# Attention with query tiles in pairs and values 512 queries wide, its order written out from the last linear head to the MLP

## The chip, the cores and the metric

The kernel runs on one core of one Trainium2 chip. The metric is the device time of one execution in microseconds (us). Before the change it was 739.01 us, the median of 3 runs (738.43 to 739.06). The engines are named as in the profile: PE (TensorE, matmuls), PEld (its weight loads), DVE (VectorE), ACT (ScalarE), POOL (GpSimd) and SP (SyncE, which here only starts DMA transfers). The five engines run side by side, each works through its own queue in order, and they wait for each other through semaphores. SBUF is the working memory, PSUM the memory that PE writes its results to.

## What is computed

One transformer block on 512 tokens of width 1024: a projection, two mixers side by side (a gated linear attention of 4 heads, and a softmax attention of 8 heads with a low-rank query and key-value path), an output projection, an MLP with a squared ReLU of width 4096, and a last normalisation. Everything is float32. Cut to what matters here:

```python
def reference(x, ...):
    n = rmsnorm(x, g_mix)
    (gq, gk, gv, gr, z_gf, z_gb, cq, ckv, kr, z_ma, z_mb) = split(n @ w_in)
    y_gla = gla_branch(gq, gk, gv, gr, z_gf, z_gb, ...)      # 4 linear heads
    y_mla = mla_branch(cq, ckv, kr, positions, ...)          # 8 softmax heads
    merged = sigmoid(z_ma) * y_gla + sigmoid(z_mb) * y_mla
    h = x + merged @ w_out
    m = rmsnorm(h, g_mlp)
    h = h + square(relu(m @ w_ff1)) @ w_ff2
    return rmsnorm(h, g_final)

def attend(qblk):                    # per head: 96 wide queries and keys, 128 wide values
    s = einsum('bhqd,bhkd->bhqk', qblk, kt)
    p = softmax(s, axis=-1)
    return einsum('bhqk,bhkv->bhqv', p, vt)
```

## The kernel before

**Arithmetic.** A float32 matrix product is made from three matmuls (`mm3`, L87): each operand is split into a high part (a rounded copy, made by ACT) and a low part (the difference, made by DVE or POOL), and high x high, high x low and low x high are added in PSUM. `split` and `split_scaled` (L92 to L98) make the two parts. So most steps appear as: PE writes a bank, ACT copies the high part, DVE subtracts, PE uses both. The names of the tiles end in h and l for the parts.

**Stages.** The first projections and three linear heads fill the time to about 255 us. Then come the last linear head, the latent products of the softmax attention, the gates zb5 to zb7 and the first unit of weights (L1310 to L1346); the attention loop over 8 heads with 4 query tiles of 128 queries each (L1369 to L1453); the output projection, written as seven products of 2x2 blocks (`wo_product`, tiles wox, wow, woz, L1790 to L1858); the row normalisation and transposes (tiles ms, mb, mr, mh, ml) that lead to the MLP; and the MLP, in four quarters of a first (f) and a second (g) product, with a table of places (`PLACES`) for its steps. `last_rows` (L1745) ends the kernel.

**The attention loop.** In turn n it makes the scores of tile n (`att_scores`, L1095: 3 matmuls of 512 keys into tile s, DVE's maximum top, ACT's exponential e with its sum tot), normalises a pair of tiles (`att_normalise`, L1110: DVE's reciprocal of tot, then ACT scales the even tile and DVE the odd one), transposes tile n-3 (`att_flip`, L1116: four transposes into tile tp, then the split into pT, high by ACT and low by DVE) and, every second turn, multiplies with the values (`att_values`, L1127). A pT tile holds 256 queries, so each head has two halves, and each of their matmuls is 256 queries wide. `merge` (L1143) then adds the head to the linear branch: DVE makes tb, POOL the halves mx and my. `up_units` (L1023) is a generator that makes the queries q, keys kbuf and values v of two heads (a pair) in between; q is one tile with high and low part side by side, and `rotary_rows` (L1044) copies the rotated rows into it with SP's transfers. The streamed weights of the output projection (tiles bo10, bo11, bo20 and so on, 1024 columns each) and the first operands for it (ga, gh, gl) are split between the turns.

**PSUM.** There are eight banks in two groups of four, under the tags at and mm. Scores and transposes use the at banks; the values, the latent products and half of the output projection the mm banks.

**Order.** The program is traced first and a scheduler then sets the order on each engine. Edges that need no semaphore pin it: `in_program_order` (L110) keeps the traced order on the engines named, and `goes_behind` (L125) puts one group behind another. Before, DVE and ACT follow the traced order up to the last linear head, PE up to the gates; from there to the output projection the scheduler decides, with some dozen `goes_behind` edges; from L1790 on, PE, ACT and DVE follow the traced order, POOL does from the attention loop on, and SP from the first step of the MLP on. `last_rows` is pinned on all engines by itself.

**The tail.** `last_rows` takes the last product in parts, and per row tile i: `out_first` squares one half on ACT, `out_mean` scales that sum on POOL, `out_gained` multiplies the right half by the gains on POOL, `out_square` squares the left half on ACT, `out_rstd` adds on DVE and takes the power -1/2 on POOL, `out_left` makes the left half on DVE, `out_right` scales the right one on ACT, and `out_store` sends both.

## Time and profile before

| What | us |
|---|---|
| median of 3 runs | 739.01 |
| the profiled execution, its own time | 739.02 |
| its span, first to last instruction | 737.3 |
| PE busy | 726.9 |
| DVE busy | 625.0 |
| ACT busy | 494.2 |
| POOL busy | 220.7 |

The span leaves out what lies around the program, some 1.7 us. Busy times of PE hold the modelled ends of matmuls, which overlap: a matmul is listed with 0.28 to 0.48 us though the next one starts sooner. How long PE is really held by one is read from the distance between two starts. "L88 PE MATMUL av<-pT,v" is an instruction of line 88 that writes tile av and reads pT and v; numbers in tile names are left out where many are grouped. An arrow in brackets names what ended an engine's idle time. The granted clock of PE was 0.998 of the full one.

### The profile page before, as it was taken

Reading aid. Unit: us, or ns where it says so; the run is one execution under the profiler, and the core shown is the slowest. Engines: PE = TensorE matmul, PEld = TensorE weight load, DVE = VectorE, ACT = ScalarE, POOL = GpSimd, SP = SyncE. Lnnn points to the kernel's source line nnn. Section 1 sums busy time; section 2 is a strip of 40 time slices with the busy share of each in tenths; the row PEclk is TensorE's granted clock in tenths of the full one; section 3 lists DMA queues with packets and bytes.
Section 4 is the critical chain, followed back from the end, with each engine's and each line's share of the span. In section 5 each row is a group of like instructions: output and inputs, shape, how many; then the busy total and the mean of one; then the engine's idle time right before and its main releaser. Section 6 shows DMA issues by size and latency. Waiting matters only on the chain.

```text
span 737.3 us, 11473 instructions
## 1 busy us (share of the span) xinstructions
PE 726.9 (99%) x4226; PEld 643.1 (87%) x4226; DVE 625.0 (85%) x861; ACT 494.2 (67%) x809; POOL 220.7 (30%) x284
## 2 busy tenths in 40 slices
PE   9999999999999999999999999999999999999995
PEld 7888888888888888899888899889988998899984
DVE  7777787889988788798898889998699869987896
ACT  7557465595696675988856879545874477537764
POOL 0732020243743724126852511200211012101215
PEclk9999999999999999999999999999999999999999
DMA  9849682431222324557978899862987088815773
GB/s 309 277 100 215 215 188 90 79 64 31 58 58 58 51 72 89 127 111 214 291 145 233 133 267 185 184 204 63 250 181 192 20 240 175 196 57 146 170 114 114
DMA packets 80520, 109.95 MB, mean 149 GB/s; under 512 B 15920, under 2 KB 34352, under 8 KB 80464
## 3 DMA queue, kind: packets, MB, share of 16 engines
q1 hardware_dynamic: 63088, 75.64, 32.9%
q0 software_dynamic: 17088, 33.30, 27.1%
q8 instruction: 33, 0.54, 0.3%
q10 hardware_dynamic: 288, 0.28, 0.1%
q14 instruction: 23, 0.19, 0.1%
HBM read 104.22 MB, written 2.10 MB: 144 GB/s over the span
## 4 chain that ended last, share of the span: by engine, by line
PE 88%; DVE 5%; issue 2%; POOL 2%; ACT 1%; DMA 1%; POOLq 0%; DVEq 0%; ACTq 0%
PE first L326 3%; PE tp L1122 2%; PE zb L88 1%; PE zb L89 1%; PE zb L90 1%; PE f2x L90 1%; PE f3x L90 1%; PE f1x L90 1%; PE f3x L89 1%; PE f2x L89 1%; PE f1x L89 1%; PE f1x L88 1%; PE f3x L88 1%; PE f2x L88 1%; PE av L89 1%
## 5 line engine op out<-in xcount | busy, mean ns | idle before, releaser
L1626 POOL DMA_DIRECT2D w<-in_w_ff x40 | 48.3, 1240 | 254.9 <-DMA w<-in_w_ff 139.3
L1102 DVE TENSOR_REDUCE top<-s 128x1 f32<-128x512 f32 x32 | 21.6, 682 | 4.9 <-PE s L90 4.7
L1107 ACT ACTIVATE e<-s,top 128x512 f32<-128x512 f32 x32 | 21.9, 687 | 3.5 <-DVE top L1102 2.6
L94 DVE TENSOR_TENSOR pT<-tp,pT 128x512 fp32r<-128x512 f32 x32 | 21.8, 682 | 2.4 <-ACT pT L93 2.0
L93 ACT ACTIVATE pT<-tp 128x512 fp32r<-128x512 f32 x32 | 19.0, 595 | 3.2 <-PE tp L1122 3.2
L1122 PE MATMUL tp<-ident,e 128*128 128x128 f32 x128 | 19.4, 274 | 0.0
L88 PE MATMUL av<-pT,v 128*128 128x256 f32 x64 | 19.1, 299 | 0.0
L90 PE MATMUL av<-pT,v 128*128 128x256 f32 x64 | 18.2, 285 | 0.0
L89 PE MATMUL av<-pT,v 128*128 128x256 f32 x64 | 18.1, 284 | 0.0
L1122 PEld LDWEIGHTS tp<-ident,e 128*128 128x128 f32 x128 | 15.2, 140 | 3.1 <-ACT e L1113 0.7
L94 POOL TENSOR_TENSOR qF<-qk,qF 128x512 fp32r<-128x512 f32 x4 | 6.6, 1641 | 37.6 <-ACT qF L93 37.6
L667 POOL DMA_DIRECT2D gvw<-in_w_in x4 | 4.8, 1230 | 38.7 <-DVE gvw L672 34.0
L667 POOL DMA_DIRECT2D zaw<-in_w_in x4 | 4.9, 1228 | 32.7 <-DVE zaw L672 28.0
L1628 DVE TENSOR_TENSOR w<-w,w 128x1024 f32<-128x1024 f32 x12 | 14.4, 1220 | 0.1
L980 POOL DMA_DIRECT2D w<-in_w_out x10 | 12.2, 1400 | 6.5 <-DVE bo60l L94 5.3
L88 PE MATMUL s<-kbuf,q 96*128 96x512 f32 x32 | 14.1, 439 | 0.0
L1153 POOL TENSOR_TENSOR mx<-tb,yg 128x256 f32<-128x256 f32 x8 | 7.7, 964 | 19.8 <-DVE tb L1150 13.9
L577 ACT ACTIVATE bds<-bd 128x512 f32<-128x512 f32 x4 | 2.4, 597 | 15.8 <-PE bd L555 15.8
L89 PE MATMUL s<-kbuf,q 96*128 96x512 f32 x32 | 12.6, 395 | 0.0
L90 PE MATMUL s<-kbuf,q 96*128 96x512 f32 x32 | 12.6, 393 | 0.0
L1113 ACT ACTIVATE e<-e,tot 128x512 f32<-128x512 f32 x16 | 11.6, 726 | 1.3 <-DVE tot L1112 1.3
L89 PEld LDWEIGHTS av<-pT,v 128*128 128x128 f32 x64 | 12.2, 191 | 0.2
(2156 smaller groups left out, 3250.4 us busy)
## 6 DMA issues: line engine op xcount, KB each, us to landing
w<-in_w_ff SPq DMA_DIRECT2D x48, 512.0 KB, 5.6
w<-in_w_ff POOLq DMA_DIRECT2D x40, 512.0 KB, 6.2
w<-in_w_out POOLq DMA_DIRECT2D x10, 512.0 KB, 8.3
grw<-in_w_in SPq DMA_DIRECT2D x8, 512.0 KB, 8.6
zaw<-in_w_in SPq DMA_DIRECT2D x8, 512.0 KB, 7.4
gvw<-in_w_in SPq DMA_DIRECT2D x8, 512.0 KB, 4.7
w<-in_w_out SPq DMA_DIRECT2D x16, 256.0 KB, 5.6
w220f<-in_w_ff SPq DMA_DIRECT2D x8, 512.0 KB, 6.2
```

Source lines behind the costliest of these rows:

```text
L88: nc.tensor.matmul(acc, lh, rh, start=start, stop=False, skip_group_check=onto)
L89: nc.tensor.matmul(acc, lh, rl, start=False, stop=False, skip_group_check=onto)
L90: nc.tensor.matmul(acc, ll, rh, start=False, stop=stop, skip_group_check=onto)
L93: nc.scalar.activation(hi, src, AF.Copy)
L94: rest.tensor_tensor(lo, src, raw(hi), op=ALU.subtract)
L326: nc.tensor.matmul(f_accs[i], a[:, i * P : (i + 1) * P], b, start=k == 0 and x == 0, stop=k == KD - 1 and x == 2)
L980: nc.gpsimd.dma_start(d, rows.rearrange("(k t p) w -> p t k w", t=2, p=P)[:, x // 2], accum_op=ALU.add)
L1102: nc.vector.tensor_reduce(top, acc, axis=AX.X, op=ALU.max, negate=True)
L1107: nc.scalar.activation(e, acc, AF.Exp, bias=top, accum_out=tot[:, qt % 2 : qt % 2 + 1])
L1122: nc.tensor.transpose(tp[:, k * P : (k + 1) * P], e[:, k * P : (k + 1) * P], ident)
L1626: nc.gpsimd.dma_start(d, self.source(src, g), accum_op=ALU.add)
L1628: nc.vector.tensor_tensor(d, d, self.tiles(src)[g], op=ALU.add)
```

## The change

Three things change together.

*Attention.* `att_flip` takes two query tiles of a head at once and fills a bank with the transposes of two key tiles for both; a pT tile now holds two key tiles of all 512 queries. `att_values` then multiplies with all 512 queries of a head at once, except for the last head, which keeps its two halves. The high and low parts of q become two tiles of their own (tag u2 in place of u4), so every SP copy into q is made twice, once for each part.

*Order.* `nc` is wrapped: from the last linear head to the last step before the MLP's table, compute and DMA calls are held under a name made of the engine's letter (P, A, D, G for POOL, S) and the tile that they write, and then issued in the order of a written sequence of 1483 entries ("P:uv00*12" is the next twelve held PE calls on tile uv00). `in_program_order(written)` pins this order on all five engines up to the end of the kernel. All `goes_behind` edges of that stretch go.

*Tail.* In `last_rows`, `out_mean` of rows 2 and 3 both go ahead of `out_gained` of row 2, and the small sum for row 3 goes behind the last addition.

```diff
+class Held:
+    ENGINES = {"tensor": "P", "scalar": "A", "vector": "D", "gpsimd": "G", "sync": "S"}
...
+    def emit(self, sequence):
+
+        held, self.held = self.held, None
+        for entry in sequence.split():
+            name, _, count = entry.partition("*")
+            for _ in range(int(count or 1)):
+                what, args, options = held[name].pop(0)
+                what(*args, **options)
...
@@ -1045,12 +1086,13 @@
             for x in range(2):
                 at = NOPE + x * HALF
-                nc.sync.dma_start(raw(qs[i][at : at + HALF]), raw(ro[x][h : h + HALF]))
+                for y in range(2):
+                    nc.sync.dma_start(raw(qs[i][y][at : at + HALF]), raw(ro[x][h : h + HALF, y]))
...
-        qs = [u4(f"q{pr}{i}") for i in range(2)]
+        qs = [[u2(f"q{pr}{i}{y}", F32R) for y in range(2)] for i in range(2)]
...
-            split_scaled(qs[0][:, 0, :], qs[0][:, 1, :], accq, QK_SCALE)
-            nc.sync.dma_start(raw(qs[1][0:64]), raw(qs[0][64:128]))
+            split_scaled(*qs[0], accq, QK_SCALE)
+            for y in range(2):
+                nc.sync.dma_start(raw(qs[1][y][0:64]), raw(qs[0][y][64:128]))
...
@@ -1113,32 +1156,30 @@
-    def att_flip(head, qt):
-        e = probs.pop((head, qt))
-        if qt % 2 == 0:
-            pTs[head, qt // 2] = [u4(f"pT{head}{qt}{x}", F32R, (P, NT, 256)) for x in range(2)]
-        tp = ps("at", f"tp{head}{qt}")
-        for k in range(NT):
-            nc.tensor.transpose(tp[:, k * P : (k + 1) * P], e[:, k * P : (k + 1) * P], ident)
-        hi, lo = pTs[head, qt // 2]
-        c = slice((qt % 2) * P, (qt % 2 + 1) * P)
-        split(hi[:, :, c], lo[:, :, c], tp.rearrange("p (k q) -> p k q", k=NT))
-
-    def att_values(head, half):
+    def att_flip(head, half):
         if half == 0:
+            pTs[head] = [[u4(f"pT{head}{x}{k}") for k in range(2)] for x in range(2)]
+        es = [probs.pop((head, 2 * half + i)) for i in range(2)]
+        cols = slice(half * HT, (half + 1) * HT)
+        for g, (hi, lo) in enumerate(zip(*pTs[head])):
+            tp = ps("at", f"tp{head}{half}{g}")
+            for i, e in enumerate(es):
+                for k in range(2):
+                    at = k * HT + i * P
+                    nc.tensor.transpose(tp[:, at : at + P], e[:, (2 * g + k) * P : (2 * g + k + 1) * P], ident)
+            split(hi[:, :, cols], lo[:, :, cols], tp.rearrange("p (k q) -> p k q", k=2))
+
+    def att_values(head, halves_):
+        if head not in avs:
             avs[head] = ps("mm", f"av{head}")
...
+        cols = slice(halves_[0] * HT, (halves_[-1] + 1) * HT)
         for k in range(NT):
             vt = vs[k // 2]
-            mm3(acc[:, half * 256 : (half + 1) * 256], vt[:, 0, k % 2, c], vt[:, 1, k % 2, c],
-                hi[:, k, :], lo[:, k, :], k == 0, k == NT - 1)
...
+            mm3(avs[head][:, cols], vt[:, 0, k % 2, c], vt[:, 1, k % 2, c],
+                his[k // 2][:, k % 2, cols], los[k // 2][:, k % 2, cols], k == 0, k == NT - 1)
+        merge(head, avs[head], halves_)
...
+    in_program_order(fixed, SPLITTERS)
+    in_program_order(ordered, PE_ONLY)
+    in_program_order(pooled, (mybir.EngineType.Pool,))
+    nc.hold()
+    written = traced()
     h = GH - 1
...
@@ -1757,8 +1761,9 @@
             out_first(i)
+        out_mean(2)
+        out_mean(3)
         out_gained(2)
-        out_mean(2)
         add_rows(2, 0, acc)
...
         out_square(3, cols[0])
-        out_mean(3)
         out_gained(3)
         out_left(1)
         out_right(1)
         out_store(1)
+        last_part(1)
         p = hparts[3]
         nc.vector.scalar_tensor_tensor(p[:, 2:3], p[:, 1:2], 1.0 / D, p[:, 2:3], op0=ALU.mult, op1=ALU.add)
-        last_part(1)
         out_square(3, cols[1], 0)
...
+    SEQUENCE = """
+        S:wr0f*2 S:zb6f A:cos A:zb6h D:cqc0 S:wr1f S:wr0f D:cqc1 D:zb6l P:bd*4 A:bds S:wr1f A:sin P:sc1*5 S:wq0f
...
+        D:ckvhl1 G:wk0l P:zb6*24 D:ro0 S:q111 P:gla3o0*12 S:wq2f S:q000 P:gla3o0*6 S:q011 A:gla3sq S:q001 A:wk1h
+        S:w2_00 P:gla3o1*6 A:zb7h D:zb7l P:uq0*9 A:q000 D:ro1 S:wq1f S:q010 A:gla3sq S:q011 A:gla3sq P:uk0*6 S:q000
+        A:gla3sq S:wq2f A:wk1h S:q001 G:gla3ss G:wk1l A:kbuf1 S:wq1f A:kbuf0 G:gla3ss A:q010 G:gla3ss G:wk1l S:wq2f
+        D:grc S:q010 G:wk1l D:grb S:q110 D:q011 S:wk2f D:grb D:kbuf0 S:q210 D:q001 S:wq1f S:q110 D:kbuf1 S:w2_10
+        P:zb7*24 D:grc S:kbuf3 S:kbuf2 P:s01*3 S:kbuf1 P:uv00*12 A:v00 P:s00*3 A:wq2h D:top00 A:wq1h G:wq2l D:zb6
+        A:e00 P:uv01*12 D:v00 G:wq1l A:wk2h S:bo10f A:wk2h P:s02*3 S:w2_11 D:top02 P:s03*3 G:wk2l S:bo11f D:top01
...
+        S:w2_01 G:mx0 P:tp301*4 D:tot32 A:pT301 S:bo21f P:s40*3 A:tb7 D:top40 A:e32 D:e33 P:uk3*6 D:pT310 A:e40
+        P:av2 D:pT311 A:q310 P:s43*3 A:q300 D:top43 P:s41*3 S:w2_01 D:top41 A:e43 P:s42*3 S:w2_21 D:top42 A:e41
+        P:tp311*4 S:w2_20 P:s52*3 A:e42 S:w2_00 D:tot40 D:q311 S:q310 A:e40 P:s50*3 D:top52 S:q301 A:pT301
+        P:tp310*4 S:w2_31 D:tot42 D:top50 A:pT300 S:q300 G:w2_21 D:pT311 A:e50 P:av2*5 D:e41 A:e52 P:av2*5 D:pT310
...
+        P:wox1*3 P:wox0*2 D:pT611 G:w2_21 P:av5 D:pT610 P:tp610*4 A:pT600 P:av5*2 D:bo20l P:tp611*4 A:pT601
+        P:tp700*4 D:top73 A:ghyo1 S:w220f D:pT610 A:ghzo0 G:glyo1 A:e73 D:pT611 S:h2 P:av5*9 D:bo50l A:pT700 P:av6
+        G:mx2 D:tot72 D:tb5 S:w2_00 D:pT710 G:mx2 D:e73 P:av6*11 G:zo1 A:gao2 P:tp701*4 A:e72 D:gao2 G:my2 P:av7*5
+        A:bo21h D:tb6 P:wow1*3 A:pT701 P:tp710*4 G:mx3 P:tp711*4 D:pT711 G:yo2 A:gao3 P:wox0*3 A:pT700 D:gao3
+        G:w2_20 P:wox1*3 A:pT701 D:bo21l A:ghzo1 P:wox0*3 G:yo2 P:av7*7 G:my3 A:ghyo2 D:tb7 P:wox1*3 G:mx3 D:h1
+        P:wow1*3 G:glzo0 D:pT711 A:gao3 P:wow0*3 A:bo51h D:pT710 P:wow0*3 D:h0 G:w2_11 A:f010h P:woz1*3 D:bo51l
...
+        S:w2_11 A:ms1 D:hp0 D:gdo0 G:hp0 D:bo40l A:ms0 S:w2_30 P:wox0*12 A:bo41h D:ms0 D:ms1 P:wox1*6 P:mb03*2 D:h3
...
+        D:h3 G:hp2 A:mh1 D:ml1 A:ms3 D:ml1 A:mr20 G:hp3 P:wox0*12 G:w2_01 A:mr20 D:h2 A:ms3 A:f020h A:ms2 D:f020l
+        A:mh2*2 D:hp2 D:ml2 G:hp2 D:hp3 D:ms2 G:hp3 D:ms3 D:ml2 A:f051h D:f021l D:f051l G:w2_01 G:w2_10 G:w2_11
+    """
+    nc.emit(SEQUENCE)
...
-    stepped = traced()
     for _, _, what, args in sorted(steps, key=lambda x: x[:2]):
         what(*args)
-    in_program_order(begun, PE_ONLY + SPLITTERS)
-    in_program_order(stepped, SP_ONLY)
-    in_program_order(attending, (mybir.EngineType.Pool,))
     last_rows(g3)
+    in_program_order(written)
```

136 lines of the change are left out of this document (71 added, 65 removed).

## Prediction

> **What bounds the kernel now.** I read the page first, then the busy time by stretches, the chain of waits, and the order of time on TensorE (PE).
>
> ```profile
> span 737.3 us, 11473 instructions
> ...
> PE 726.9 (99%) x4226; PEld 643.1 (87%) x4226; DVE 625.0 (85%) x861; ACT 494.2 (67%) x809; POOL 220.7 (30%) x284
> ...
> PE 88%; DVE 5%; issue 2%; POOL 2%; ACT 1%; DMA 1%; POOLq 0%; DVEq 0%; ACTq 0%
> ```
>
> PE is busy for 99% of the span and makes 88% of the chain that ended last. So an edit counts if it shortens PE's own stream, closes a gap in it, or shortens what follows the last matmul. The other engines count only where PE waits for them. The change touches the stretch from about 255 us to the start of the MLP near 412 us, and the tail. Three stretches of it, with the columns PE, weight loads, DVE, ACT, POOL (busy us and count), then clock and DMA:
>
> ```profile
> 254.80:302.00 47.20, 47.20 (x275) 41.47 (x274) 37.01 (x64) 32.12 (x67) 13.93 (x18) 1.00 0.37 93
> 302.00:374.00 72.00, 72.00 (x496) 65.24 (x495) 63.54 (x113) 62.37 (x138) 40.01 (x48) 1.00 0.68 180
> 374.00:413.00 39.00, 38.91 (x185) 31.98 (x184) 35.75 (x51) 24.87 (x44) 14.50 (x16) 1.00 0.91 202
> ```
>
> In the attention stretch (302 to 374) DVE is idle 8.5 of 72 us and ACT 9.6, but in the output projection (374 to 413) DVE is busy 35.75 of 39 us. The chain of waits says the same: between 255 and 690 us it leaves PE once for long, and then runs for the most part on DVE, from the first row below to the second, until PE takes over in the third.
>
> ```profile
> 383.60 1.24 DVE bo51l L94
> ...
> 419.32 1.14 DVE f021l L1620
> ...
> 421.12 0.38 PE f0w L89
> ```
>
> Three gaps of PE in the order of time (start, duration):
>
> ```profile
> 285.21 0.28 PE L90 MATMUL uv<-wk0h,ckvhl 128*128 128x256 f32 x1
> 285.43 0.39 PE L88 MATMUL uv<-wk0h,ckvhl 128*128 128x256 f32 x1
> 285.65 0.28 PE L89 MATMUL uv<-wk0l,ckvhl 128*128 128x256 f32 x1
> ...
> 406.67 0.39 PE L88 MATMUL wox<-bo40h,gdo 128*128 128x512 f32 x1
> 407.14 0.50 PE L89 MATMUL wox<-bo40l,gdo 128*128 128x512 f32 x1
> 407.48 0.39 PE L90 MATMUL wox<-bo40h,gdo 128*128 128x512 f32 x1
> ...
> 420.71 0.28 PE L88 MATMUL f0w<-mh,f021h 128*128 128x256 f32 x1
> 421.12 0.38 PE L89 MATMUL f0w<-ml,f021h 128*128 128x256 f32 x1
> 421.33 0.28 PE L90 MATMUL f0w<-mh,f021l 128*128 128x256 f32 x1
> ```
>
> **The change part by part.** What one matmul really takes is the distance between starts, since durations overlap. Between the first row below and the second lie 12 matmuls 512 wide, between the second and the third 23 of 256:
>
> ```profile
> 722.85 0.39 PE L88 MATMUL ge<-g340h,f3h 128*128 128x512 f32 x1
> ...
> 725.57 0.28 PE L88 MATMUL gend<-g340h,f3h 128*128 128x256 f32 x1
> ...
> 728.32 0.28 PE L90 MATMUL gend<-g341h,f3l 128*128 128x256 f32 x1
> ```
>
> So a 512-wide one costs 2.72 / 12 = 0.227 us and a 256-wide one 2.75 / 23 = 0.1196 us. Laid over the gaps: 285.21 to 285.65 holds two 256-wide ones, 0.44 - 0.24 = 0.20 us lost; 406.67 to 407.48 two 512-wide ones, 0.81 - 0.45 = 0.36; 420.71 to 421.33 two 256-wide ones, 0.62 - 0.24 = 0.38. That is 0.94 us in all.
>
> *Values 512 wide.*
>
> ```profile
> L88 PE MATMUL av<-pT,v x64: 278/283/367, 306.9 to 374.4; 128*128 128x256 f32 x64
> L1122 PE MATMUL tp<-ident,e x128: 270/272/331, 299.5 to 370.4; 128*128 128x128 f32 x128
> ```
>
> The values make 64 matmuls on each of three lines, 192 of 256 columns. Afterwards heads 0 to 6 make 7 x 12 = 84 of 512, and the last head keeps its 24 of 256. Each of the 84 replaces two: 2 x 0.1196 - 0.227 = 0.0125 us, times 84 = 1.05 us off PE's stream. The transposes stay 128 of the same size, and the copies that split them still move 128x512 each, so query pairs cost and save nothing there. One bound is that PE waits elsewhere for what it saves here (0), the other is 1.05. I take 1.05 here and give the loss to a rival.
>
> [...]
>
> *The written order, attention and output projection.* No compute instruction is added or changes its engine here; only places in the queues move. What matters is which late thing PE meets. In the old order the splits of the streamed output weights (bo20l, bo21l, bo50l) and of the merged rows (gao) stand behind the last split of a flip on DVE; in the written sequence bo20l, bo50l, gao2, bo21l and the first half of gao3 stand ahead of the last one (D:pT710). Three splits of 1024 columns at the 1.24 us of bo51l's row are 3.7 us, moved from the stretch where DVE has 3.3 us free into the one where it has 8.5. bo40l goes ahead of both scaled rows (D:bo40l, D:ms0, D:ms1), while its products move behind the transposes mb. So the gaps at 407 and 421 should close. The one at 285 goes too if only because the uv products now follow the first scores. Bounds of this part: all three closed, -0.94; from the other side each of 32 flip groups and 32 score groups has a producer that could come late, and the nearest row for how late is the stretch of an e on DVE, 0.67 us, worked out with the rivals below. I take -0.9, nearest to closing, since DVE's free time in the receiving stretch is twice what it is given.
>
> *Query rows in separate tiles.* High and low parts of q become two tiles, so each copy of rotated rows to a head is two transfers.
>
> ```profile
> L1048 SPq DMA_DIRECT2D q<-ro x16: 507/544/591, 282.6 to 327.5; - x16
> ...
> DMA to landing us min/median/max: 2.2/2.4/3.5
> ```
>
> The 16 become 32, and the 2 copies inside the middle pairs become 4: 18 more issues at 0.544 us, 9.8 us of SP's queue over about 110 us. I cost them at nothing on the path. The cover is the zb7 block: the last q copy of pair 0 stands ahead of 24 matmuls 512 wide, 24 x 0.227 = 5.4 us, and a copy lands 2.4 us after issue; without it the first scores would come 2 x 0.544 = 1.1 us later for each of 4 pairs, 4.4 us. Behind a copy that waits on SP stand weight loads of later pairs, which are needed a whole pair later.
>
> *The tail.* out_mean of row 3 goes ahead of out_gained of row 2 on POOL, and the small sum for row 3 goes behind the last addition on DVE.
>
> ```profile
> 726.35 0.67 DVE L1465 TENSOR_TENSOR h<-h,ge 128x512 f32<-128x512 f32 x1
> 727.35 0.75 DVE L1734 SCALAR_TENSOR_TENSOR ms<-h,hp,gfin 128x512 f32<-128x512 f32 x1 [0.33 <-POOL hp L1730]
> ...
> 728.42 0.75 DVE L1734 SCALAR_TENSOR_TENSOR ms<-h,hp,gfin 128x512 f32<-128x512 f32 x1
> ...
> 729.88 0.16 DVE L1776 SCALAR_TENSOR_TENSOR hp<-hp 128x1 f32<-128x1 f32 x1 [0.71 <-POOL hp L1717]
> 729.96 0.42 DVE L1754 TENSOR_TENSOR h<-gend,h 128x256 f32<-128x256 f32 x1
> 730.29 1.45 DVE L1734 SCALAR_TENSOR_TENSOR ms<-h,hp,gfin 128x512 f32<-128x512 f32 x1
> 732.47 0.75 DVE L1734 SCALAR_TENSOR_TENSOR ms<-h,hp,gfin 128x512 f32<-128x512 f32 x1 [0.66 <-POOL hp L1730]
> 726.40 0.19 ACT L1713 ACTIVATION_READ_ACCUMULATOR ms<-h 128x1 f32 x1
> 729.66 0.19 POOL L1717 TENSOR_SCALAR hp<-hp 128x1 f32<-128x1 f32 x1
> 729.93 1.26 POOL L1720 TENSOR_TENSOR ms<-h,gfin 128x512 f32<-128x512 f32 x1
> 731.89 0.55 POOL L1730 TENSOR_TENSOR hp<-hp,mhalf 128x1 f32<-128x1 f32 x1 [0.69 <-DVE hp L1727]
> ```
>
> The last matmul ends at 728.60, but the last addition starts at 729.96: DVE stands 0.71 us at the small sum (729.88), which waits for out_mean on POOL (729.66). After the change the addition can start when out_left of row 1 ends, 728.42 + 0.75 = 729.17, 0.79 us earlier. But out_left of row 2 took 1.45 us against 0.75, exactly while POOL ran out_gained (729.93 to 731.19). Now out_mean of row 3 cannot start before 726.59 (ACT's row), so out_gained of row 2 starts at about 726.9, just ahead of out_left of row 0 (726.35 + 0.67 = 727.0, its power being done earlier), which it holds to 728.2; out_left of row 0 ends at 728.9, the sum and power of row 2 (0.55) at 729.9, out_left of row 1 at 730.0, out_gained of row 3 at 731.3, out_left of row 2 at 732.0, the last power at 732.7. Against 732.47 that is +0.2. If no two collide: the addition 0.79 and out_left of row 2 0.70 earlier, -1.5 together. I take +0.1, nearest to the collision, since the same two instructions still meet.
>
> The sum on the profiled execution, 739.02 us (span 737.3 and 1.7 around it; the median shown, 739.01, is the same): -1.05 - 0.9 + 0.1 = -1.85, so **737.2 us**.
>
> **The rivals.** *Slower: four banks and longer runs.* Scores and flips share four PSUM banks. The old order puts matmuls of another kind after every two or so of them; the written one has seven in a row with one other matmul among them (s43, s41, s42, tp311, s52, s50, tp310) and one of five. With 3 x 0.227 us for a score and 0.44 for a flip (first row), PE comes back to the first bank after about 1.8 us, and the reduction and the exponential that free it take 0.68 + 0.69. That leaves less than 0.45 us for a late DVE.
>
> ```profile
> 299.68 0.44 PE tp L1122 x4
> ...
> L1102 DVE TENSOR_REDUCE top<-s x32: 669/680/692, 294.1 to 365.9; 128x1 f32<-128x512 f32 x32
> L1107 ACT ACTIVATE e<-s,top x32: 668/687/707, 294.8 to 366.9; 128x512 f32<-128x512 f32 x32
> L1114 DVE TENSOR_SCALAR e<-e,tot x16: 477/504/1176, 298.9 to 368.0; 128x512 f32<-128x512 f32 x16
> ```
>
> The reduction of a score, which reads PSUM, hardly varies (692 at most for a median of 680), but the normalisation e ranges up to 1176 ns, 0.67 over its median. If it stretches in five of the runs of four or more, PE loses 5 x 0.67 = 3.4 us; the values still save 1.05: 739.0 + 2.3 = 741.3. It decides from three such runs on (2.0 - 1.05 against the 0.9 that stays). Against it: PE lost nothing of that size here before.
>
> [...]
>
> *Given back.* DVE owns the chain from 383 to 421. If the splits moved ahead of D:pT710 only delay those of the flips, PE saves 1.05 in the values and waits as long in the projection: at most 0.9 less is left over, at least nothing, 738.4. For it speaks the 35.75 of 39; against it the 8.5 free before. [...]
>
> *The tail gains too.* No collision there: 739.0 - 1.05 - 0.9 - 1.5 = 735.6. For it speaks that the two starts are 0.1 us apart; against it, out_gained of row 3 still has to fit.
>
> **How the numbers follow.** Forecast 0.50, given back 0.18, tail 0.16, slower 0.16. What a measurement of this kernel can tell is 0.2%, 1.5 us: faster is below 737.5, slower above 740.5. The forecast's own range is 736.4 (half of the tail's 1.5 won) to 738.0 (half the gaps stay, 0.3 more in the tail); 0.43 of its 0.50 lies below 737.5. With the tail's 0.16 and 0.01 of giving back, faster is 0.60. Slower is 0.16 and 0.01 for more waits than I see, 0.17; the rest, 0.23, is the same. The range goes from 735.0 (the tail's case with 0.6 more from smaller gaps) to 740.8, which leaves most of the slower case out, 0.12, and about 0.05 below.
>
> **What would show it.** Right: 84 value matmuls of 512 columns about 0.227 us apart; no distance over 0.3 us between matmuls from 285 to 421; the chain on PE there; the first MLP matmul about 2 us earlier than before. Wrong: PE starting a score or a flip late behind e or a split of a flip; first scores waiting for a q transfer; in the tail, out_left of row 2 at 0.75 instead of 1.45 us, or the last ACT scale starting more than 4.1 us after the last matmul. The forecast falls if PE's waits in the stretch sum to over 2 us.

## The result, and the profile after

After the change the kernel takes 740.55 us (median of 16 runs, 739.82 to 742.02), before it 738.87 us (16 runs beside them, 738.28 to 739.55). The ratio is 1.0025, 95% interval 1.0017 to 1.0033: slower by 1.7 us, where the forecast had 1.85 us faster (739.02 to 737.2). Among all runs below, one execution was slow, 2655.61 us in the experiment "apart + q and k splits + two", whose ratio is of the others. The profiled execution took 741.22 us. Its page, answering to the lines quoted of before:

```profile
span 739.5 us, 11335 instructions
...
PE 90%; DVE 4%; ACT 2%; DMA 1%; issue 1%; POOL 0%; SPq 0%; POOLq 0%; DVEq 0%; ACTq 0%
```

The last two of the three stretches shown of before, by their busy times (columns as before: PE, weight loads, DVE, ACT, POOL, then clock, DMA share, GB/s):

```profile
302.00:374.00 72.00, 72.00 (x418) 61.79 (x417) 63.97 (x115) 62.88 (x135) 33.87 (x38) 1.00 0.70 187
374.00:413.00 39.00, 37.84 (x179) 30.14 (x178) 37.60 (x49) 25.10 (x43) 18.77 (x19) 1.00 0.70 149
```

The attention stretch still holds PE without a break. In the output projection PE is idle 1.16 us of 39, where it was 0.09, and DVE, the engine that was nearly full there, is busy for 37.60 instead of 35.75. The distance between two marks of PE's stream says where the time went: the first score of the last linear head and the first MLP matmul, in before's order of time, then in after's.

```profile
255.41 0.36 PE L88 MATMUL sc<-qk,qk 128*128 128x256 f32 x1
...
412.50 0.28 PE L88 MATMUL f0x<-mh,f010h 128*128 128x256 f32 x1
```

```profile
254.85 0.36 PE L76 MATMUL sc<-qk,qk 128*128 128x256 f32 x1
...
413.43 0.28 PE L90 MATMUL f0x<-mh,f010h 128*128 128x256 f32 x1
...
443.83 0.28 PE L90 MATMUL f0x<-mh,f071l 128*128 128x256 f32 x1
445.49 0.36 PE L90 MATMUL f0x<-mh,f040h 128*128 128x256 f32 x1 [1.38 <-DVE f0a L90]
...
730.47 0.28 PE L90 MATMUL gend<-g341h,f3l 128*128 128x256 f32 x1
```

From mark to mark it was 157.09 us and is now 158.58, 1.5 more. From the first MLP matmul to the last it was 315.82 (728.32 - 412.50) and is 317.04, 1.2 more, and the row at 445.49 holds all of that, 1.66 us behind its neighbour where 0.12 is usual, less the 0.38 of the gap at 421. From the last matmul to the end of the span there are 9.0 us in both. The first mark itself stands 0.56 us earlier, behind the same 1244 matmuls; over the traces of this case it lies between 254.68 and 255.91, so this is no gain of the change. Together that is the 2.2 us between the two profiled executions (741.22 and 739.02).

The old gaps at 285, 407 and 421 us are gone. In their place, up to the MLP, PE has these (in the order of time):

```profile
288.77 1.33 PE L76 MATMUL s<-kbuf,q 96*128 96x512 f32 x3
289.94 0.29 PE L76 MATMUL uv<-wk0h,ckvhl 128*128 128x256 f32 x1
...
377.23 0.39 PE L76 MATMUL wow<-bo20h,gao 128*128 128x512 f32 x1
378.10 0.47 PE L76 MATMUL woz<-bo50h,ghyo 128*128 128x512 f32 x1 [0.49 <-DVE pT L76]
...
388.73 0.39 PE L76 MATMUL woz<-bo51l,ghbo 128*128 128x512 f32 x1
389.62 0.50 PE L76 MATMUL woz<-bo51h,glbo 128*128 128x512 f32 x1 [0.50 <-DVE glbo L76]
...
394.09 0.39 PE L76 MATMUL woz<-bo30h,ghzo 128*128 128x512 f32 x1
...
398.01 0.39 PE L76 MATMUL woz<-bo30h,ghzo 128*128 128x512 f32 x1
```

Less 0.227 us for each 512-wide matmul, the four places lose 0.49 (three matmuls in 1.17), 0.64 (one in 0.87), 0.66 (one in 0.89) and 1.20 us (twelve in 3.92): 3.0 us. Less the 0.56 us of the gaps at 285 and 407 and the 0.87 that the values save (below) that makes 1.6, against 1.5 by the marks. What DVE did before each of the last three, with what GpSimd did at the same time below it:

```profile
372.95 3.48 DVE L76 TENSOR_TENSOR bo21l<-bo21f,bo21h 128x1024 fp32r<-128x1024 f32 x1
...
383.31 1.99 DVE L76 TENSOR_TENSOR yo<-my 128x256 f32<-128x256 f32 x1
...
386.96 0.41 DVE L76 TENSOR_TENSOR yo<-yo,mx 128x256 f32<-128x256 f32 x1
...
391.82 2.52 DVE L76 TENSOR_TENSOR bo30l<-w,bo30h 128x1024 fp32r<-128x1024 f32 x1
...
394.87 1.21 DVE L76 TENSOR_TENSOR bo31l<-w,bo31h 128x1024 fp32r<-128x1024 f32 x1
```

```profile
372.69 1.19 POOL L76 DMA_DIRECT2D w<-in_w_out  x1
373.46 1.18 POOL L76 TENSOR_TENSOR yo<-yo,mx 128x256 f32<-128x256 f32 x1
374.17 1.16 POOL L76 TENSOR_TENSOR my<-tb,yg 128x256 f32<-128x256 f32 x1
...
383.06 1.19 POOL L76 DMA_DIRECT2D w<-in_w_out  x1
383.83 1.18 POOL L76 TENSOR_TENSOR zo<-mx,yo 128x256 f32<-128x256 f32 x1
...
390.25 1.68 POOL L76 DMA_DIRECT2D w<-in_w_out  x1
391.01 2.25 POOL L76 TENSOR_TENSOR glzo<-zo,ghzo 128x512 fp32r<-128x512 f32 x1
```

bo21l took 3.48 us and bo30l 2.52, where a split of that size takes 1.21 (bo31l); yo took 1.99 where its sister takes 0.41. Each ran beside GpSimd operations that follow each other without a break (a DMA_DIRECT2D is GpSimd's part in starting a load), and ended 1.1, 0.3 and 1.1 us after the last of them (375.33, 385.01, 393.26). The waits at 377 and 389 us and those from 394 on follow: pT behind bo21l on DVE, glbo behind yo, and bo31l, glzo and glco behind bo30l. Summed over the rows from 285 to 425 us, DVE's instructions that took over 0.1 us more than the lower quartile of their form took about 8 us more; in before it was about 4, and none took over 0.7 more. Not every such meeting goes this way: bo51l, in the same trace, began at 379.07 us, 0.31 behind a load and 0.47 ahead of GpSimd's zo, as bo21l had begun 0.26 behind and 0.51 ahead; it took only 1.62 us and ended before zo did (381.29).

### The profile page after: what moved, and what is told of

Same layout as the page of the kernel before. It is cut to its first block, busy times and chain, and to the rows that moved or that the text cites. A ratio compares the mean times of both kernels' runs of the same rounds, so it can differ in the third digit from the quotient of the medians.

```text
span 739.5 us, 11335 instructions
## 1 busy us (share of the span) xinstructions
PE 726.6 (98%) x4142; PEld 637.5 (86%) x4142; DVE 628.1 (85%) x861; ACT 494.8 (67%) x809; POOL 222.8 (30%) x284
## 4 chain that ended last, share of the span: by engine, by line
PE 90%; DVE 4%; ACT 2%; DMA 1%; issue 1%; POOL 0%; SPq 0%; POOLq 0%; DVEq 0%; ACTq 0%
PE f3x L90 3%; PE f2x L90 3%; PE f1x L90 3%; PE first L90 3%; PE g2x L90 3%; PE g1x L90 3%; PE g0x L90 3%; PE gvx L90 3%; PE zax L90 3%; PE grx L90 3%; PE s L76 3%; PE gk L90 2%; PE cq L90 2%; PE gq L90 2%; PE zb L90 2%; PE g3x L90 2%
## 5 line engine op out<-in xcount | busy, mean ns | idle before, releaser
L76 PE MATMUL s<-kbuf,q 96*128 96x512 f32 x96 | 28.0, 408 | 0.1
L76 PE MATMUL av<-pT,v 128*128 128x512 f32 (+1 forms) x108 | 25.1, 372 | 0.0
L76 PEld LDWEIGHTS av<-pT,v 128*128 128x128 f32 x108 | 18.6, 189 | 3.4 <-ACT pT L76 0.2
L76 PEld LDWEIGHTS s<-kbuf,q 96*128 96x128 f32 x96 | 16.6, 189 | 3.3 <-DVE q L76 0.4
L76 PE MATMUL tp<-ident,e 128*128 128x128 f32 x128 | 17.4, 272 | 0.0
L76 POOL TENSOR_TENSOR my<-tb,yg 128x256 f32<-128x256 f32 x8 | 7.8, 970 | 23.5 <-DVE tb L76 23.4
L90 ACT ACTIVATE f0h<-f0a 128x512 fp32r<-128x512 f32 x10 | 6.1, 621 | 6.2 <-DVE f0a L90 6.2
L90 ACT ACTIVATE f3h<-f3a 128x512 fp32r<-128x512 f32 x10 | 6.1, 620 | 6.2 <-DVE f3a L90 6.2
```

Of the source, the lines that this page charges most:

```text
L76: what(*args, **options)
L90: return what(*args, **options)
```

## The experiments

Each was run in five rounds beside the kernel before, whose median in the groups was 738.6 to 739.1 us. "Changed" is the kernel after, the order its written sequence; an entry D:x is the next instruction of VectorE that writes tile x (A ScalarE, G GpSimd, S SyncE, P TensorE). Edits of the sequence are cut to the entries that move and their neighbours. Two rows can be told apart where their intervals do not overlap; the changed kernel itself has 1.0025 (1.0017 to 1.0033).

| Experiment | us | to before, 95% interval |
|---|---|---|
| before + wide values, no written order | 741.51 | 1.0035 (1.0022 to 1.0047) |
| the same, values two tiles later | 740.27 | 1.0018 (1.0009 to 1.0027) |
| changed, values 256 wide | 741.32 | 1.0033 (1.0021 to 1.0046) |
| changed, tail as before | 740.19 | 1.0016 (1.0007 to 1.0024) |
| MLP splits and transfers, first order | 743.63 | 1.0065 (1.0051 to 1.0079) |
| MLP transfers, second order | 741.70 | 1.0048 (1.0035 to 1.0062) |
| MLP transfers, one entry | 740.24 | 1.0017 (1.0009 to 1.0026) |
| first q and k splits ahead | 740.15 | 1.0022 (1.0013 to 1.0032) |
| VectorE and GpSimd apart, four entries | 738.79 | 1.0001 (0.9992 to 1.0010) |
| twelve entries at once | 744.29 | 1.0075 (1.0062 to 1.0087) |
| three edits together | 739.68 | 1.0017 (1.0009 to 1.0026) |
| apart + q and k splits + two | 739.34 | 1.0004 (0.9995 to 1.0014) |
| apart + one transfer | 738.67 | 1.0002 (0.9993 to 1.0011) |
| apart, f010l later | 738.15 | 0.9993 (0.9984 to 1.0001) |
| the same, two splits and one transfer | 737.90 | 0.9988 (0.9979 to 0.9997) |
| the same, one more swap | 738.18 | 0.9991 (0.9982 to 1.0000) |

### What the width of the values is worth

```diff
-            mm3(avs[head][:, cols], vt[:, 0, k % 2, c], vt[:, 1, k % 2, c],
-                his[k // 2][:, k % 2, cols], los[k // 2][:, k % 2, cols], k == 0, k == NT - 1)
+            for x in halves_:
+                q = slice(x * HT, (x + 1) * HT)
+                mm3(avs[head][:, q], vt[:, 0, k % 2, c], vt[:, 1, k % 2, c],
+                    his[k // 2][:, k % 2, q], los[k // 2][:, k % 2, q],
+                    k == 0 and x == halves_[0], k == NT - 1, True)
```

> The changed kernel with each 512-wide value product of heads 0 to 6 issued as two of 256, at the same places of the written order; pairs of tiles, banks and order stay. Width worth 1.05 us: 740.55 + 1.05, about 741.6. Rival, the width is worth nothing because what follows waits for the split chain anyway: 740.4 to 740.8.

It took 741.32 us, 0.8 more than the changed kernel beside its own runs of before (ratios 1.0033 and 1.0025, with intervals that overlap). The counts in the sequence go with it (P:av1*24 for P:av1*12). The traces put a number on it, free of what follows: from the second score to the first product of the output projection (first the changed kernel, then this one, order of time on PE) stand the value products of five heads, and no wait over 0.11 us in either.

```profile
291.38 0.40 PE L76 MATMUL s<-kbuf,q 96*128 96x512 f32 x1
...
357.58 0.39 PE L76 MATMUL wox<-bo10h,gao 128*128 128x512 f32 x1
```

```profile
291.70 0.40 PE L76 MATMUL s<-kbuf,q 96*128 96x512 f32 x1
...
358.52 0.40 PE L76 MATMUL wox<-bo10h,gao 128*128 128x512 f32 x1
```

That is 66.20 us and 66.82: 0.62 us for 5 x 12 = 60 wide matmuls, 0.0103 each, 0.87 us for the 84. So the width is worth 0.9 us and not 1.05, and the loss is not in it.

Alone, the same width in the kernel before, with pairs of flips (`att_flip` and `att_values` as in the change):

```diff
-        if 0 <= b < 4 * MH:
+        if 0 <= b < 4 * MH and b % 2:
             flips = traced()
-            att_flip(b // 4, b % 4)
+            att_flip(b // 4, b % 4 // 2)
```

> The kernel before with the flips in pairs and the values 512 queries wide, and nothing else of the change: no written order, query tiles as before. If the values are worth what the step for them said (84 matmuls by 0.0125 us) and the loss of the change sits in the written order: 738.9 - 1.05, about 737.8 us, 737.3 to 738.4. Rival, the four transposed banks and longer runs cost more than the width gives: 738.9 us or more, about 741 by the rival's own price, with new PE waits between 292 and 365 us.

741.51 us: the rival's sign, but by a cause of another kind. The scheduler put the first value product right behind the flips of its own head. In the order of time on PE, and the stretch from 308 us (columns as above):

```profile
306.43 0.40 PE L90 MATMUL s<-kbuf,q 96*128 96x512 f32 x1
308.39 0.50 PE L88 MATMUL av<-pT,v 128*128 128x512 f32 x1 [1.55 <-ACT pT L93]
...
309.82 0.63 PE L89 MATMUL av<-pT,v 128*128 128x512 f32 x1
310.25 0.63 PE L90 MATMUL av<-pT,v 128*128 128x512 f32 x1
```

```profile
308.00:312.00 4.00, 3.61 (x10) 2.84 (x11) 3.07 (x5) 3.05 (x6) 0.76 (x2) 0.61 0.59 178
```

PE waited 1.55 us for pT, and then ran for some 3.4 us with 0.43 us from one 512-wide matmul to the next instead of 0.227; the granted clock of that stretch is 0.61. Wait and clock cost 3.4 us together: eleven 512-wide matmuls took the 5.94 us from 306.43 to 312.37. Asked for two tiles later (with the merged sums that read them), the products lose that:

```diff
-        if c >= 0 and (c % 4 == 3 or c == 4 * MH - 3):
+        if c in (5, 9, 13, 17, 21, 25, 27, 29):
             valued = traced()
-            att_values(c // 4, (0, 1) if c // 4 < MH - 1 else (0,))
+            att_values((c - 2) // 4 if c < 27 else c // 4, (0, 1) if c < 29 else (0,))
```

> The kernel before with the flips in pairs and the values 512 wide, as in the first experiment, and the value products of heads 0 to 5 asked for two score tiles later, so that they don't stand right behind the flips that they wait for. Theory, the wait of 1.6 us at 306 us, the lower granted clock that followed it (0.61 from 308 to 312 us) and the two waits at 352 and 360 us came from that place alone, and the width is worth 0.8 to 1.05 us with no written order: 737.8 to 738.2. Rival, pairs of flips hold banks and splits so long that the planner's order loses wherever the values stand: 739 or more.

740.27 us, the rival again. The wait at 306 and the low clock were gone, but PE waited anew at 344, 352, 360 and 374 us, 0.4 to 0.8 each. In these two orders of the scheduler the pairs of flips lose more than the width gives; in the written one they do not.

### What the tail is worth

```diff
-        out_mean(2)
-        out_mean(3)
         out_gained(2)
+        out_mean(2)
         add_rows(2, 0, acc)
```

> The changed kernel with the last rows in the order of the kernel before: on VectorE and ScalarE the mean of row group 3, the gain of row group 2 and one part of the last product back in their places. The traces of before and after have the same 9.0 us from the last matmul to the end, so the edit of the tail is worth nothing: 740.55, 740.2 to 740.9. By the term of the sum, 0.1 less than after: 740.45. Rival, the tail gave up to 0.7: 741.2.

740.19 us, nothing that can be told apart by the times. The traces can: from the last matmul to the end of the span there are 8.90 to 9.00 us in the four traces with the old tail, and 9.05 to 9.18 in the fourteen with the new one, so the new tail is longer by 0.05 to 0.3. In the changed kernel out_left of row 0 took 1.84 us (728.98) beside out_gained of row 2, as the forecast had it, and the two instructions that the forecast let meet later did meet: out_left of row 2 on DVE, and out_gained of row 3 on GpSimd.

```profile
732.33 1.75 DVE L90 SCALAR_TENSOR_TENSOR ms<-h,hp,gfin 128x512 f32<-128x512 f32 x1
```

```profile
732.27 1.26 POOL L90 TENSOR_TENSOR ms<-h,gfin 128x512 f32<-128x512 f32 x1
```

### Taking VectorE and GpSimd apart

Four entries are moved. bo21l goes behind two splits that PE needs first, GpSimd's zo2 ahead of a load, f010l behind glbo3, and glzo1 between two loads, where DVE adds from PSUM:

```diff
-A:pT701 D:bo21l A:ghzo1
+A:pT701 A:ghzo1
-D:h0 G:w2_11
+D:h0 D:bo21l G:w2_11
-G:w2_10 D:yo3 P:wow0*3 D:bo60l P:woz0*3 G:zo2 P:wow1*3
+G:zo2 G:w2_10 D:yo3 P:wow0*3 D:bo60l P:woz0*3 P:wow1*3
-D:zo3 D:f010l P:woz1*3
+D:zo3 P:woz1*3
-D:glbo3 G:w2_00
+D:glbo3 D:f010l G:w2_00
-G:w2_20 P:wox1*3 D:h1 P:woz1*3 G:glzo1 D:h3
+G:glzo1 G:w2_20 P:wox1*3 D:h1 P:woz1*3 D:h3
```

> The changed kernel with four entries moved, all for VectorE and GpSimd between 370 and 395 us: bo21l behind pT711 and pT710; GpSimd's zo2 ahead of the load beside it; f010l behind glbo3; GpSimd's glzo1 between two loads, where VectorE reads PSUM. Theory, VectorE stands still while GpSimd works through several operations (bo21l 3.48 us, yo3 1.99, bo30l 2.52 where 1.21, 0.41, 1.21 is usual), and TensorE's waits at 377, 389 and 394 to 398 us, 0.7 + 0.8 + 1.2, are that: 740.55 - 2.4, about 738.2, 737.6 to 739.0. Rival, the operations stretch whatever they meet, as bo60l did for 3.36 us in the combined order: another wait in place of each, 740.0 or more.

738.79 us, equal to before: 1.8 us come back from four places in a queue, with no instruction fewer. The marks agree: 157.11 us from the first score to the MLP, 1.5 less than in the changed kernel. VectorE's excess, summed as above, falls from about 8 us to 3.9, with bo21l at 1.28 us, yo at 0.96 and bo30l at 1.91. That bo21l stood ahead of the splits was not the harm by itself: VectorE now idles 1.87 us at that place (until 375.47), more than the 1.21 of a split that is not held. At 389 us the two causes are not parted, since f010l's 1.22 us went from ahead of glbo as well.

Before that, twelve entries were moved at once, with glzo1 right behind the load that follows zo2:

```diff
-D:yo3 P:wow0*3 D:bo60l
+D:yo3 P:wow0*3 D:bo60l G:glzo1
```

> The four entries above and eight more: on VectorE bo21l behind the two splits pT711 and pT710; q and k splits of the first head pair ahead of grc and grb; on GpSimd zo2 ahead of the load beside it and glzo1 ahead of the two loads that it stood behind. Theory, four stalls of the written order carry the loss and none of the rest does: 1.6 (443 us), 0.7 (377), 0.5 (289) and 0.8 + 1.1 (389 to 398) less, 740.55 - 4.7, about 735.9, 735.2 to 736.8. Rival, VectorE is the bound from 370 to 400 us and gives the stalls back elsewhere: only the first and third count, 738.4 or more.

744.29 us. The waits from 394 to 398 us were gone, and 1.0 us stood at 388 instead, for bo60l; the one for glbo stayed (0.7 us at 391). DVE and GpSimd in that kernel:

```profile
385.58 3.36 DVE L76 TENSOR_TENSOR bo60l<-w,bo60h 128x1024 fp32r<-128x1024 f32 x1
```

```profile
385.33 1.20 POOL L76 DMA_DIRECT2D w<-in_w_out  x1
386.11 1.75 POOL L76 TENSOR_TENSOR glzo<-zo,ghzo 128x512 fp32r<-128x512 f32 x1
```

In both orders the stall stands where glzo falls on a split. The rest of that run's loss came with the edits of the MLP and of the first splits, below. In the fastest order of all (its section is the last of these), bo21l, bo30l and glzo stand so:

```profile
379.21 1.27 DVE L76 TENSOR_TENSOR bo21l<-bo21f,bo21h 128x1024 fp32r<-128x1024 f32 x1
...
389.69 0.68 DVE L76 TENSOR_TENSOR h<-h,wow 128x512 f32<-128x512 f32 x1
390.29 0.68 DVE L76 TENSOR_TENSOR h<-h,woz 128x512 f32<-128x512 f32 x1
391.08 1.23 DVE L76 TENSOR_TENSOR bo30l<-w,bo30h 128x1024 fp32r<-128x1024 f32 x1
```

```profile
374.68 1.18 POOL L76 TENSOR_TENSOR yo<-yo,mx 128x256 f32<-128x256 f32 x1
...
379.34 1.74 POOL L76 TENSOR_TENSOR zo<-mx,my 128x256 f32<-128x256 f32 x1
...
389.73 1.29 POOL L76 TENSOR_TENSOR glzo<-zo,ghzo 128x512 fp32r<-128x512 f32 x1 [1.91 <-ACT ghzo L76]
```

glzo runs beside two additions that read PSUM, and neither is longer (0.68, 0.68; the fourteen of this form in the changed kernel took 0.67 to 0.69); bo30l after it takes 1.23. bo21l began 0.13 us before GpSimd's zo and was not held; zo was (1.74; yo, of the same size and also right behind a load, took 1.18 while DVE was idle). The recorded starts do not settle which of the two is held, though: bo21l and yo in the changed kernel and bo60l above began 0.5 us ahead of GpSimd's tensor operation, behind the load alone, and were held all the same.

### The transfers of the first MLP block

f041h waits for its accumulating load in the changed kernel, and not in the run with the old tail, which is the same up to there (ScalarE of both):

```profile
442.43 1.06 ACT L90 ACTIVATE f041h<-w 128x1024 fp32r<-128x1024 f32 x1 [1.98 <-DMA w<-in_w_ff]
```

```profile
440.16 1.05 ACT L90 ACTIVATE f041h<-w 128x1024 fp32r<-128x1024 f32 x1
```

GpSimd issued that load at 432.31 and 432.24 us, so it landed about 10 us later in the one and within 8 in the other. The one profile took 741.22 us, the other 739.37. Six traces have these loads in this order. In two, this one and that of "apart + q and k splits + two", the load landed 10.0 and 9.5 us after its issue, and PE waited; in the four others it landed after 7.2 to 7.8 and PE did not. So the wait stands in some executions only, which fits the sixteen times of the changed kernel: they spread over 2.2 us, where those of before spread over 1.3, and five lie above 741. The transfers start later, as one stretch shows (before, then after; the last two numbers are the share of the transfer engines and GB/s):

```profile
408.00:412.00 4.00, 4.00 (x19) 3.33 (x18) 3.66 (x6) 3.62 (x9) 0.47 (x2) 1.00 1.00 175
```

```profile
408.00:412.00 4.00, 4.00 (x19) 3.30 (x19) 4.00 (x5) 4.00 (x10) 1.02 (x1) 1.00 0.00 1
```

In before, GpSimd issued the load that waits for f011l at 405.80 us, the one that waits for f050l at 412.57, and three more from 416.94 on. Now f050l's goes first, at 410.98, and f011l's follows at 413.84, because VectorE splits f011l at 410.20 instead of 404.14. That load landed at 420.25 instead of 412.36; f051h on ScalarE had waited 3.10 us for it, and the next three loads went out from 422.94 on. So the transfer engines are idle at 408 and half used at 420 (0.51, before 1.05), and full (0.87 to 1.13, before 1.04 to 1.13) from 424 to 444. Three edits tried it. The first moved splits too:

```diff
-D:bo40l A:ms0 S:w2_30
+D:f011l G:w2_01 D:bo40l A:ms0 S:w2_30
-D:h2 A:ms3 A:f020h
+D:h2 A:ms3 A:f051h A:f020h
-A:f051h D:f021l D:f051l G:w2_01
+D:f051l D:f021l G:w2_01
```

> The changed kernel with four entries of the written order moved: on VectorE f011l ahead of bo40l and f051l ahead of f021l, on ScalarE f051h ahead of f020h, on GpSimd the accumulating load that waits for f011l right behind it, ahead of the one that waits for f050l. Theory, the 1.6 us wait of the first MLP block for f041h at 443.8 us comes from that load standing behind another in GpSimd's queue: the wait goes, 740.55 - 1.6, about 738.9, 738.5 to 739.5. Rival, the transfer is late because the queues are full, or the next block of the MLP waits in its place: 740.2 or more, with the wait at 443 or a new one before 480.

743.63 us, a miss: f011l, put ahead of bo40l, held the normalised rows, and PE waited 1.1 us for them at 406, 0.6 at 420, and 0.9 for f021l at 424; 0.6 of the old wait was left, at 447. The second left PE's producers in place:

```diff
-D:f050l A:mr11 A:mr21 A:ms2 D:f011l G:w2_00
+D:f011l G:w2_01 D:f050l A:mr11 A:mr21 A:ms2 G:w2_00
-G:hp3 D:ms3 D:ml2 A:f051h D:f021l D:f051l G:w2_01 G:w2_10 G:w2_11
+G:hp3 G:w2_10 D:ms3 D:ml2 A:f051h D:f021l G:w2_11 D:f051l G:w2_01
```

> The changed kernel with the transfers of the first MLP block in another order on GpSimd, and one swap on VectorE: f011l ahead of f050l, the accumulating load that waits for f011l ahead of the one that waits for f050l, and the two that wait for f020l and f021l ahead of the one that waits for f051l. The splits that TensorE waits for keep their places (the first edit of this kind moved them, and the wait went to them). Theory, the wait of 1.6 us at 443.8 us is a late transfer that comes late in about half of the executions (the sixteen times of the changed kernel go from 739.8 to 742.0 us): median 739.8 to 740.2, all runs within 1.3 us, no wait over 0.3 us between 421 and 480. Rival, the transfers are late from the number queued and not from their order: 740.5 or more, spread of 2 us.

741.70 us, a miss as well. The wait at 443 was gone and one of 0.9 us stood at 434, since the load for f061h, now behind two others, landed late (ScalarE):

```profile
432.84 1.06 ACT L90 ACTIVATE f061h<-w 128x1024 fp32r<-128x1024 f32 x1 [3.60 <-DMA w<-in_w_ff]
```

The third moves one entry, a load of 512 KB into the time when the queue was half empty:

```diff
-G:hp3 D:ms3 D:ml2 A:f051h D:f021l D:f051l G:w2_01 G:w2_10 G:w2_11
+G:hp3 G:w2_10 D:ms3 D:ml2 A:f051h D:f021l D:f051l G:w2_01 G:w2_11
```

> The changed kernel with one entry moved: on GpSimd the accumulating load that waits for f020l ahead of the one that waits for f051l. Theory, the wait of 1.6 us at 443.8 us, which stands in some executions only, is a queue of 512 KB transfers: three are issued together at 422.9 us while the transfer engines are half idle (share 0.51 from 420 to 424 us), and the one for f041h stands behind them. With one of the three at 419.2 us the wait goes from every execution: median 739.8 to 740.2, none over 740.9. Rival, the loads that SyncE issues from 435.5 us on are in its way: as before, 740.5 with times up to 742.

740.24 us, and none of eleven runs over 740.91. The load for f041h now landed 5.9 us after its issue, and within 5.8 to 6.0 in the three further traces with this one entry moved. That is the queue's part in the loss: about 0.3 us of the median, less than the intervals can tell, and the long times (five of sixteen over 741 in the changed kernel). With the four entries it brings nothing more that can be told apart:

> The four entries moved for VectorE and GpSimd between 370 and 395 us (738.8), and that one entry of the MLP transfers. If the wait at 443.8 us is in none of its executions already: no change, 738.6 to 738.9. If it is in some: 738.4, with a spread under 1.2 us.

738.67 us.

### The first scores, and what came next

The wait at 289 us is for a split of q. VectorE had stood 3.35 us at grc, ahead of it in the queue, until GpSimd's gla3ss came (286.27). VectorE's order, and e00 on ScalarE:

```diff
-D:grc D:grb D:q011 D:grb D:kbuf0 D:q001 D:kbuf1
+D:q011 D:kbuf0 D:q001 D:kbuf1 D:grc D:grb D:grb
-A:wq1h G:wq2l D:zb6 A:e00
+G:wq2l D:zb6 A:e00 A:wq1h
```

> The changed kernel with the q and k splits of the first head pair ahead of grc and grb on VectorE, and on ScalarE e00 ahead of wq1h, whose weight arrived late in the combined order. Theory, the wait at 289 us (0.48) is VectorE held at grc by GpSimd's gla3ss: 740.55 - 0.45, about 740.1. Rival, the next wait is the weights' arrival at 293 us: 740.5 or more, with a wait of 0.4 us or more between 293 and 312.

740.15 us, the theory's number, but its interval overlaps that of the changed kernel, and the trace does not bear the theory out: the wait at 289 us was gone, and PE waited 0.9 us at 308.8, for a copy of rotary rows into a q tile (the row's bracket names it):

```profile
309.76 0.47 PE L76 MATMUL s<-kbuf,q 96*128 96x512 f32 x1 [0.72 <-DMA q<-ro]
```

So in this execution the 0.5 us and more went to the next arrival, one of the transfers of which the change makes twice as many. All three edits together:

> The edits of the last three together. Theory, they add: 740.55 - 0.5 - 2.4 - 0.45, about 737.2, 736.6 to 738.2, faster than the kernel before by 1.0 or more. Rival, each gives its gain to a next limit: 739 or more.

739.68 us; the MLP edit's wait for f061h, 0.9 us at 432, is what it lacks against 738.8. And with SyncE's copies pulled ahead:

```diff
-S:q101 D:top13 S:q211 S:bo11f
+S:q101 S:q100 S:q101 D:top13 S:q211 S:bo11f
-D:bo30l A:bo31h P:wox1*6 A:gdo0 D:h2
+A:bo31h P:wox1*6 A:gdo0 D:h2 D:bo30l
```

> The edits of the run with four entries moved between 370 and 395 us (738.8) and of the run with the first q and k splits ahead (740.15), without those of the MLP transfers, and two more: bo30l on VectorE behind one more addition that reads PSUM, and the last two copies of rotary rows into the q tiles of head 2 ahead of five loads on SyncE, because the wait of 0.9 us at 308.8 us was for them. Theory, the waits add: 738.8 - 0.4 for 289 us, the wait at 308 us does not appear in its place, and 0.6 less at 395 us: 737.8, 737.2 to 738.5. Rival, the next arrival or VectorE's own length takes it back: 738.7 or more.

739.34 us, a miss: the waits at 289 and 395 us were gone, but that at 309 us stayed (0.7 us, now for a pT split), and that at 443 us was in the profiled execution.

### An order that is faster than before

f010l behind glco3, its load and reader with it, and ghzo1 behind ms0:

```diff
-A:ms0 D:glbo3 D:f010l G:w2_00
+A:ms0 A:ghzo1 D:glbo3
-A:bo30h G:glzo1 G:w2_20
+A:bo30h G:w2_20 G:glzo1
-D:glco3 A:bo70h
+D:glco3 D:f010l G:w2_00 A:bo70h
-A:bo41h D:ms0
+A:bo41h A:f050h D:ms0
```

> The four entries moved between 370 and 395 us, and with them f010l with its load behind glco3 (its reader f050h behind bo41h), and ScalarE's ghzo1 behind ms0, so that GpSimd's glzo1 falls on VectorE's additions that read PSUM. Theory, from 388 to 398 us VectorE's own work is the bound (waits of 0.6 us in all at 395 us are left in 738.8), and 1.2 us of split taken out of it is worth those 0.6: 738.2. Rival, the transfer that waits for f010l is needed sooner, and a wait comes back between 404 and 425 us: 738.8 or more.

738.15 us. The waits at 395 us went, but with f010l's 1.2 us the last 0.7 us of stretch left bo30l too, so this run doesn't part VectorE's length from its collisions. A wait of 0.6 us came at 411.8, because ScalarE stood 1.5 us at f050h. Moving f021h into that time, f011l ahead of f050l, and the one MLP transfer:

```diff
-A:bo41h A:f050h
+A:bo41h A:f021h A:f050h
-D:h2 A:f021h D:f050l A:mr11 A:mr21 A:ms2 D:f011l
+D:h2 D:f011l D:f050l A:mr11 A:mr21 A:ms2
```

> The last order (738.15) with the one entry of the MLP transfers, and two more: ScalarE's f021h in the place where it stood idle for f050h's transfer (1.5 us before 406.4), and f011l ahead of f050l on VectorE. Theory, the wait of 0.6 us at 411.8 us that came with f010l's later place is ScalarE held by that idle time, and goes: 738.15 - 0.6, about 737.5, 737.0 to 738.0, with a ratio below 1 by more than its interval. Rival, the transfers of 404 to 425 us are needed where they stood: 738.2 or more.

737.90 us, ratio 0.9988 (0.9979 to 0.9997): faster than the kernel before by 0.8 us, and than the changed one by 2.6 by the medians. It is the best of the orders tried, and its interval ends just below 1; the marks are the firmer sign:

```profile
255.91 0.36 PE L76 MATMUL sc<-qk,qk 128*128 128x256 f32 x1
...
412.16 0.28 PE L90 MATMUL f0x<-mh,f010h 128*128 128x256 f32 x1
```

156.25 us from the first score of the last linear head to the MLP, 0.84 less than before, with the 0.5 us at 289 still in it; the runs just before and after this one have 156.26 and 156.25. One swap more, on GpSimd:

```diff
-G:w2_00 P:wox1*12
+G:w2_01 G:w2_00 P:wox1*12
```

> The same, and on GpSimd the load that waits for f011l ahead of the one that waits for f050l. Theory, both loads go earlier or at the same time: 737.5 as well, 737.0 to 738.0. Rival, what moved the wait to f061h in the second MLP order was this swap and not the two loads ahead of the last: 738.2 or more, with a wait at 432 us.

738.18 us, the same. Its profile has no wait at 432 us, and the one before it 0.4 us there; so, by one execution of each, the swap is not what made f061h late, and the loads moved ahead of the last are left.

## Why the prediction was wrong

- *Values, -1.05.* The mechanism was right, the size off: 0.87 us, since a pair saved 0.0103 us in the attention loop, where the rows of the MLP had given 0.0125.
- *The written order, -0.9.* This is the step that failed, and by the prediction's own sign (PE's waits in the stretch over 2 us) the forecast falls with it: "I take -0.9, nearest to closing, since DVE's free time in the receiving stretch is twice what it is given." The three gaps did close (0.94), and four others opened (3.0 us), so the step cost 2.1 us where it was to save 0.9; four moved entries give back 1.5 us of it by the marks, 1.8 by the times. Free time on DVE was the wrong measure. What counted was what GpSimd did in it: a split of 1024 columns placed on three GpSimd operations took 3.48 us. The forecast's row for the worst case was e, 0.67 us over its median, the largest stretch of the old order; so the bound on the loss side was too near by a factor of three (2.27 us for bo21l). The profile of before had nothing larger, though there too GpSimd worked without a break (372.8 to 376.3 us), with three splits of VectorE beside it longer by 0.5 us each: a trace bounds the collisions of the order that it shows.
- *What was not a step at all.* The transfers of the MLP were not followed past the end of the written part, though GpSimd's queue was rewritten: 1.5 us in the profiled execution, and none in others.
- *Query rows in separate tiles, 0.* Right for the changed kernel: no PE wait of it is for a q transfer. The wait at 309 us with the first splits ahead shows that the cover was thin.
- *The tail, +0.1.* Right: from the start of the last matmul to that of the last scaling it was 4.15 us (728.32 to 732.47) and is 4.34 (730.47 to 734.81), the +0.2 that the prediction worked out, with the collisions of out_left and out_gained as it had them.
- *The rivals.* "Slower: four banks and longer runs" had the sign and nearly the size (741.3), but not the cause, so that it came near is chance; the stated range (735.0 to 740.8) reaches the measured time only on this rival's account. Between 292 and 372 us PE lost 0.1 us at one place, in the run of seven that this rival names (335.6 us), and no more. In the scheduler's order the pairs did cost waits, which is the nearest that a run came to it. "Given back" named DVE's ownership of 383 to 421; the run with f010l later leaves room for 0.6 us of it at most by the times, 0.85 by the marks. No rival had GpSimd as the cause, though the longest e, which the first is priced from (1176 ns), was such a meeting: it began at 346.38 us, and GpSimd's glzo ran from 345.57 to 347.27.

Left open: what makes one transfer of 512 KB land in 7.2 us in one execution and in 10.0 in another of the same order of loads; which of VectorE and GpSimd is held when their recorded starts lie within half a microsecond (bo21l and bo51l went opposite ways); and the 0.5 us at 289, which no order here wins without a wait at 309.

## What to carry to other kernels

When VectorE and GpSimd are both reordered, lay out both queues against the same clock: where it can be helped, a split with two SBUF inputs should not fall on a run of GpSimd's operations (bo21l 3.48 us for 1.21), and an addition that reads PSUM can (0.68 beside glzo). A stretch seen in a trace holds for that order alone (bo21l took 1.21 us before, 3.48 in the changed kernel, 1.28 with four entries moved), so price a move by what it will stand beside: at worst the whole run of the neighbour, in most places here less. And an order that ends at a boundary still sets when the transfers behind it start: follow each queue to its next reader (the load that waits for f011l landed at 420.25 us instead of 412.36).

## What the runs showed of the hardware

- A VectorE instruction with two SBUF inputs that met several GpSimd operations in succession was in some places held through all of them: 3.48 and 3.36 us for 1.21, both ending 1.1 us after the last. In others it was held for less: bo51l took 1.62 us, and three splits in the kernel before 0.5 us more each.
- In the kernel before with wide values alone, after a wait of 1.55 us with one of 0.26 us shortly before it, PE's 512-wide matmuls came 0.43 us apart for about 3.4 us where 0.227 is usual (granted clock 0.61 over 4 us). The wait of 1.38 us at 443 in the changed kernel was followed by matmuls at their usual distance (256 wide, 0.12 us).
